# Layer 1's residual, scaled in pieces under the query and gate projections and added in place

## The chip, the cores and the metric

The kernel runs on one core of a Trainium2 chip. The metric is the device time of one execution in microseconds (us). Six actors matter: TensorE (PE; its weight loads are listed apart as PEld), VectorE (DVE), ScalarE (ACT), GpSimd (POOL), SyncE (SP), which here only issues transfers, and the 16 DMA engines that carry them. Each engine runs its own list of instructions in order; engines wait for each other through semaphores.

## The reference

Two layers of a decoder trunk over 256 tokens of width 2048, in float32. Layer 0 is a gated linear recurrence, layer 1 a sparse attention with a gate. Each layer ends alike, with alpha = 4 ** 0.25:

```
h = _layer_norm(alpha * h + mixer(h) @ w_out, ln_g, ln_b)

def _layer_norm(x, g, b):
    mu  = mean(x);  var = mean((x - mu) ** 2)
    return (x - mu) * rsqrt(var + 1e-5) * g + b
```

So layer 1 needs layer 0's output h twice: for its input projection, and again at its end as the residual alpha * h. What is computed of it at the end is `n * l0_ln_g + l0_ln_b`, where n is the normalised value before gain and bias.

In layer 1, `x @ w_in` gives queries (2048 columns), six groups of keys and values (512 columns each), 48 gate logits and the gate z (2048 columns). Queries and keys get a partial rotary embedding. The attention's result is multiplied by silu(z) and goes through `w_out` (2048 x 2048).

## The kernel before

**Tiles.** Tokens lie in two tiles of 128 (t = 0, 1), the width in 16 pieces of 128. A matmul in full precision is three passes: both factors are split into a high part (fp32r) and the remainder, and hi·hi, hi·lo and lo·hi are added (`tok_step`, lines 138 to 142, with 512 columns; `project_t`, lines 185 to 189, with 256). All weights pass once through one stream: `load` (line 105) issues a transfer of 512 KB on SP into a raw slot `wr`; ScalarE writes the high part `wh` (line 78), VectorE the remainder `wl` (line 79); then TensorE uses them. There are three raw slots and five pairs of split buffers, or four and eight while the pool `wide` is open. A raw slot is free again when VectorE has made the remainder. SP's list holds the loads in order, so a load that waits for a slot holds all that stand behind it.

**Stages.** Layer 0 with its norm (which writes n to a tensor `norm0` in DRAM), layer 1's keys and values, then four groups of queries: `query(g)` projects 512 columns, applies `rotary` (line 552: a copy `qr` on ScalarE, four operations on GpSimd, back into `qr`), transposes on TensorE (line 198) and does the attention; `gate(g)` projects 512 columns of z and multiplies. In this stage `wide` is closed. At last the output projection: four groups of 512 columns, the last one token tile by token tile (`project_by_tile`), each followed by `residual` (line 852: hb = alpha * xr + product) and the sums for the norm; then the norm's two steps with l1_ln_g and l1_ln_b and the stores.

**The residual before.** In the output projection, `fetch(c)` (line 820) loads 512 columns of n into `xr` (two buffers), 512 columns of gain and bias into `gb` (one buffer), all issued by SP, and GpSimd multiplies and adds (lines 828 and 829). `row` (line 832) loads l1_ln_g and l1_ln_b, 1 MB each when spread over the 128 partitions. `wide` is opened again after the second group.

**What sets the order.** A scheduler puts every engine's list in order, by a timeline of its own, from the order of the code, priorities (weight splits go up to 300 instructions ahead) and explicit rules such as `issue_after`. So a new transfer or operation can stand elsewhere in the lists than in the code.

## Time and profile before

| | |
|---|---|
| median of 3 runs | 1016.73 us (1016.64 to 1019.19) |
| profiled execution | 1017.92 us, span 1016.2 us |
| granted TensorE clock, mean | 0.994 |
| TensorE busy | 997.0 us |
| VectorE, ScalarE, GpSimd busy | 670.2, 543.9, 116.3 us |
| moved by DMA | 185.25 MB, 182 GB/s in the mean |

The span goes from the first to the last instruction. Queries, gates and attention take about 676 to 905 us of it, the output projection about 905 to 1005, the end behind the last matmul the rest. In rows of the profile a line number stands for the code, `out<-in` for the tiles, `x` for the number of instructions; "A <- B" means that A waited for B. A busy TensorE is not TensorE at its peak, since the ends of matmuls are modelled; starts are measured.

### The profile page before, as it was taken

To read this page: it belongs to the slowest core of one execution; us is meant where nothing else is said; L and a number is where in the kernel's file an instruction comes from. 1 tells how busy PE (TensorE), PEld (TensorE's weight loads), DVE (VectorE), ACT (ScalarE), POOL (GpSimd) and SP (SyncE) were. 2 spreads that over 40 slices of the span, in tenths; PEclk is the share of its full clock that TensorE was granted. 3 is DMA by queue.
4 is the path that set the end of the run, shared out by engine and by line. 5 is a ranking of instruction groups with operands and counts; after the bars stand their busy time and mean duration, and the time that the engine had idled before them with its cause. 6 is when DMAs were issued, how large, how long until landed. Compare 5 with 4: busy or idle time off the path is not lost.

```text
span 1016.2 us, 15908 instructions
## 1 busy us (share of the span) xinstructions
PE 997.0 (98%) x6041; PEld 883.4 (87%) x6041; DVE 670.2 (66%) x1101; ACT 543.9 (54%) x864; POOL 116.3 (11%) x180
## 2 busy tenths in 40 slices
PE   8999999999999999999999999999999999999995
PEld 8988998899889988878889878899989889998775
DVE  6786658665866686656575555466857668675566
ACT  6654455445544554424476545564856667775240
POOL 1400300030003000310011020101010022000540
PEclk9999999999999999999999999999999999999998
DMA  9865565556655655557465677577354454445872
GB/s 304 260 214 166 155 176 178 163 151 178 179 156 153 183 174 162 163 176 258 141 217 175 205 227 230 165 218 212 108 165 144 146 166 130 121 145 184 308 253 83
DMA packets 100781, 185.25 MB, mean 182 GB/s; under 512 B 6097, under 2 KB 20513, under 8 KB 100193
## 3 DMA queue, kind: packets, MB, share of 16 engines
q1 hardware_dynamic: 99232, 178.67, 57.7%
q0 software_dynamic: 1472, 5.56, 1.8%
q8 instruction: 47, 0.77, 0.3%
q14 instruction: 30, 0.24, 0.1%
HBM read 180.02 MB, written 4.19 MB: 181 GB/s over the span
## 4 chain that ended last, share of the span: by engine, by line
PE 86%; DMA 5%; DVE 3%; issue 3%; POOL 2%; ACT 1%; SPq 0%; POOLq 0%; ACTq 0%; DVEq 0%
PE pjb L141 15%; PE pjb L142 15%; PE pjb L140 15%; PE pjb L187 9%; PE pjb L185 9%; PE pjb L188 9%; PE mxb L425 2%; DMA wr<-in_l_w_in_dram 2%; DMA wr<-in_l_w_out_dram 2%; DVE wl L79 1%; PE mxb L198 1%; PE mxb L548 1%; PE mxb L550 1%; PE mxb L549 1%; PE mxb L777 1%
## 5 line engine op out<-in xcount | busy, mean ns | idle before, releaser
L79 DVE TENSOR_TENSOR wl<-wr,wh 128x1024 fp32r<-128x1024 f32 (+2 forms) x330 | 396.4, 1205 | 221.6 <-ACT wh L78 219.0
L78 ACT ACTIVATE wh<-wr 128x1024 fp32r<-128x1024 f32 (+2 forms) x330 | 340.4, 1036 | 350.9 <-PE pjb L142 144.8
L185 PE MATMUL pjb<-ah,wh 128*128 128x256 f32 x832 | 235.4, 284 | 1.2 <-ACT wh L78 1.2
L187 PE MATMUL pjb<-al,wh 128*128 128x256 f32 x832 | 235.7, 284 | 0.0
L188 PE MATMUL pjb<-ah,wl 128*128 128x256 f32 x832 | 234.5, 284 | 0.5 <-DVE wl L79 0.5
L141 PE MATMUL pjb<-wl,ah 128*128 128x512 f32 (+1 forms) x576 | 223.3, 388 | 0.3 <-DVE wl L79 0.3
L140 PE MATMUL pjb<-wh,ah 128*128 128x512 f32 (+1 forms) x576 | 222.8, 387 | 0.0
L142 PE MATMUL pjb<-wh,al 128*128 128x512 f32 (+1 forms) x576 | 222.8, 387 | 0.0
L185 PEld LDWEIGHTS pjb<-ah,wh 128*128 128x128 f32 x832 | 157.0, 189 | 2.2 <-ACT wh L78 1.6
L188 PEld LDWEIGHTS pjb<-ah,wl 128*128 128x128 f32 x832 | 156.2, 189 | 1.2 <-DVE wl L79 1.1
L187 PEld LDWEIGHTS pjb<-al,wh 128*128 128x128 f32 x832 | 156.2, 188 | 0.5
L142 PEld LDWEIGHTS pjb<-wh,al 128*128 128x128 f32 x576 | 109.0, 189 | 22.3
L141 PEld LDWEIGHTS pjb<-wl,ah 128*128 128x128 f32 x576 | 109.0, 189 | 22.0 <-DVE wl L79 0.6
L140 PEld LDWEIGHTS pjb<-wh,ah 128*128 128x128 f32 x576 | 108.9, 189 | 22.0
L141 PE MATMUL pjb<-wl,bh 128*128 128x512 f32 (+1 forms) x272 | 105.1, 386 | 1.4 <-DVE wl L79 1.4
L142 PE MATMUL pjb<-wh,bl 128*128 128x512 f32 (+1 forms) x272 | 104.1, 384 | 0.0
L140 PE MATMUL pjb<-wh,bh 128*128 128x512 f32 (+1 forms) x272 | 103.1, 384 | 0.2 <-ACT wh L78 0.2
L141 PEld LDWEIGHTS pjb<-wl,bh 128*128 128x128 f32 x272 | 51.3, 189 | 13.7 <-DVE wl L79 3.3
L140 PEld LDWEIGHTS pjb<-wh,bh 128*128 128x128 f32 x272 | 51.2, 188 | 11.3 <-ACT wh L78 0.6
L142 PEld LDWEIGHTS pjb<-wh,bl 128*128 128x128 f32 x272 | 51.3, 189 | 10.5
L488 POOL TENSOR_TENSOR gz<-gz,gn 128x512 f32<-128x512 f32 x8 | 13.6, 1697 | 317.4 <-ACT gz L487 316.8
L559 POOL TENSOR_TENSOR rot<-qr,cc 128x128 f32<-128x128 f32 x14 | 9.5, 679 | 275.2 <-ACT qr L555 274.9
(220 smaller groups left out, 1013.8 us busy)
## 6 DMA issues: line engine op xcount, KB each, us to landing
wr<-in_l_w_in_dram SPq DMA_DIRECT2D x230, 512.0 KB, 3.8
wr<-in_l_w_out_dram SPq DMA_DIRECT2D x64, 512.0 KB, 4.3
wr<-in_l_w_in_dram SPq DMA_DIRECT2D x16, 280.0 KB, 3.3
wr<-in_l_cmp_w_k_dram SPq DMA_DIRECT2D x8, 512.0 KB, 4.4
wr<-in_l_cmp_w_v_dram SPq DMA_DIRECT2D x8, 512.0 KB, 4.3
xr<-in_x_dram POOLq DMA_DIRECT2D x4, 512.0 KB, 6.1
norm<-hb POOLq DMA_DIRECT2D x2, 1024.0 KB, 5.4
xr<-norm SPq DMA_DIRECT2D x4, 512.0 KB, 7.4
```

Source lines behind the costliest of these rows:

```text
L78: act.activation(hi, src, AF.Copy)
L79: dve.tensor_tensor(lo, src, hi.bitcast(F32), op=OP.subtract)
L140: pe.matmul(ps, xh, wh, start=(k == 0), stop=False)
L141: pe.matmul(ps, xh, wl, start=False, stop=False)
L142: pe.matmul(ps, xl, wh, start=False, stop=(k == KT - 1))
L185: pe.matmul(o, hi[:, kk, c], xh, start=(k == 0 and b % 2 == 0), stop=False, skip_group_check=True)
L187: pe.matmul(o, hi[:, kk, c], xl, start=False, stop=False, skip_group_check=True)
L188: pe.matmul(o, lo[:, kk, c], xh, start=False, stop=(k == KT - 1), skip_group_check=True)
L198: last[0] = pe.transpose(ps[:, i], src[:, i], ident).ins
L425: pe.matmul(ps[:, h], km[:, h].rearrange("p b r j -> p (b r j)"), later, start=True, stop=True)
L488: pool.tensor_tensor(z, z, gn, op=OP.mult)
L548: pe.matmul(o, a[0], b[0], start=start, stop=False)
```

## The change

Layer 1's residual is now made in eight pieces of 256 columns. A function `rescale` is called in each of the four query and four gate projections, after the third of its eight weight tiles. It takes a raw weight slot, loads 256 columns of n (256 KB) and of gain and bias (128 KB each, spread over the partitions) into it through SP, multiplies and adds on GpSimd, and stores the 256 KB to a new DRAM tensor `res1` by GpSimd's queue. In the output projection, 512 columns at a time of `res1` are loaded straight into `hb`, and `residual` adds in place. `l1_ln_g` and `l1_ln_b` come in four pieces each. All these loads are placed by a table of (column group, weight tile), each to be issued after the weight load named last. `wide` opens after the first group instead of the second. `fetch`, `xr` and `gb` are gone.

```diff
--- before.py
+++ after.py
@@ -66,6 +66,7 @@
     mx = ctx.enter_context(tc.tile_pool(name="mx", bufs=4, space=PSUM))
     dram = ctx.enter_context(tc.tile_pool(name="dram", bufs=1, space=DRAM))
     norm0 = dram.tile([S, D], F32, name="norm0")
+    res1 = dram.tile([S, D], F32, name="res1")
 
     def pjb(shape):
         return pj.tile(shape, F32, name="pjb", tag="pjb")
@@ -99,10 +100,13 @@
         def at(self, k, c):
             return self.hi[k // 4][:, k % 4, c], self.lo[k // 4][:, k % 4, c]
 
+    queued = [None]
+
     def load(w, j, c0, n):
 
         raw = slot([128, 2, n], F32, "wr", 3, 1)
-        nc.sync.dma_start(raw, w[256 * j:256 * (j + 1), c0:c0 + n].rearrange("(k p) n -> p k n", p=128))
+        queued[0] = nc.sync.dma_start(raw, w[256 * j:256 * (j + 1), c0:c0 + n].rearrange(
+            "(k p) n -> p k n", p=128)).ins
         return raw
 
     def weights(w, j, c0, n):
@@ -153,10 +157,14 @@
                 also(j)
         return ps
 
-    def project_by_tile(xs, w, c0, after, behind=None, halve=False):
-
-
-        ws = [weights(w, j, c0, 512) for j in range(KT // 2)]
+    def project_by_tile(xs, w, c0, after, behind=None, halve=False, also=None):
+
+
+        ws = []
+        for j in range(KT // 2):
+            ws.append(weights(w, j, c0, 512))
+            if also:
+                also(j)
         for t in range(NT):
 
             n = 256 if halve and t == NT - 1 else 512
@@ -789,14 +797,30 @@
         act.activation(o, po, AF.Copy)
         return o
 
+    todo = list(range(D // 256))
+
+    def rescale(j):
+
+
+        if j != 2:
+            return
+        u = slice(256 * todo[0], 256 * todo.pop(0) + 256)
+        r = slot([128, 4, 256], F32, "wr", 3, 1)
+        nc.sync.dma_start(r[:, 0:2], norm0[:, u].rearrange("(t p) d -> p t d", p=128))
+        for i, name in enumerate(("l0_ln_g", "l0_ln_b")):
+            nc.sync.dma_start(r[:, 2 + i], a[name][None, u].to_broadcast([128, 256]))
+        for i, op in enumerate((OP.mult, OP.add)):
+            pool.tensor_tensor(r[:, 0:2], r[:, 0:2], r[:, 2 + i, None].to_broadcast([128, 2, 256]), op=op)
+        nc.gpsimd.dma_start(res1[:, u].rearrange("(t p) d -> p t d", p=128), r[:, 0:2])
+
     def query(g):
-        pq = project(hT, w1, C_Q + 512 * g)
+        pq = project(hT, w1, C_Q + 512 * g, rescale)
         q = [rotary(at, t, pq[t]) for t in range(NT)]
         ps = [scores(g, t, q[t]) for t in range(NT)]
         return [values(g, t, ps[t]) for t in range(NT)]
 
     def gate(g, os):
-        for i, ps in enumerate(project_t(hT, w1, C_Z + 512 * g)):
+        for i, ps in enumerate(project_t(hT, w1, C_Z + 512 * g, also=rescale)):
             zT = at.tile([128, 2, S], F32, name="zT", bufs=1)
             act.activation(zT, ps, AF.Silu)
             for t in range(NT):
@@ -817,40 +841,29 @@
     stats = n1.tile([128, NT, 8, 6], F32, name="stats", bufs=1)
 
 
-    def fetch(c):
+
+    g1, b1 = (n1.tile([128, D], F32, name=n, bufs=1) for n in ("g1", "b1"))
+    others = {}
+    for c, at in enumerate(((0, 5), (1, 0), (2, 0), (2, 3))):
         cs = slice(512 * c, 512 * (c + 1))
-        xr = n1.tile([128, NT, 512], F32, name="xr")
-        nc.sync.dma_start(xr, norm0[:, cs].rearrange("(t p) d -> p t d", p=128))
-        gb = n1.tile([128, 2, 512], F32, name="gb", bufs=1)
-        for i, name in enumerate(("l0_ln_g", "l0_ln_b")):
-            nc.sync.dma_start(gb[:, i], a[name][None, cs].to_broadcast([128, 512]))
-        for t in range(NT):
-            pool.tensor_tensor(xr[:, t], xr[:, t], gb[:, 0], op=OP.mult)
-            pool.tensor_tensor(xr[:, t], xr[:, t], gb[:, 1], op=OP.add)
-        return xr
-
-    def row(name):
-        r = n1.tile([128, D], F32, name=name, bufs=1)
-        nc.sync.dma_start(r, a[name][None, :].to_broadcast([128, D]))
-        return r
-
+        others[at] = hb[:, :, cs], res1[:, cs].rearrange("(t p) d -> p t d", p=128)
+        for i, (r, name) in enumerate(((g1, "l1_ln_g"), (b1, "l1_ln_b"))):
+            at = ((2, 5), (2, 7), (3, 0), (3, 1), (3, 2), (3, 3), (3, 5), (3, 7))[2 * c + i]
+            others[at] = r[:, cs], a[name][None, cs].to_broadcast([128, 512])
+
+    def also(c, j):
+        if (c, j) in others:
+            with tc.issue_after(queued[0]):
+                nc.sync.dma_start(*others[c, j])
 
     for c in range(4):
         cs = slice(512 * c, 512 * (c + 1))
 
-        xr = []
-
-        def behind(j, c=c, xr=xr):
-            if j == 3:
-                xr.append(fetch(c))
-
-        def residual(t, ps, c=c, xr=xr, parts=range(2)):
-            xr = xr[0]
+        def residual(t, ps, c=c, parts=range(2)):
             n = ps.shape[1] // len(parts)
             for i, u in enumerate(parts):
                 h = hb[:, t, 512 * c + 256 * u:512 * c + 256 * (u + 1)]
-                dve.scalar_tensor_tensor(h, xr[:, t, 256 * u:256 * (u + 1)], ALPHA, ps[:, n * i:n * (i + 1)],
-                                         op0=OP.mult, op1=OP.add)
+                dve.scalar_tensor_tensor(h, h, ALPHA, ps[:, n * i:n * (i + 1)], op0=OP.mult, op1=OP.add)
                 dve.bn_stats(stats[:, t, 2 * c + u], h)
 
         def finish(t, ps):
@@ -871,16 +884,12 @@
                     nc.sync.dma_start(y[128 * t:128 * (t + 1), gs], h)
 
         if c < 3:
-            for t, ps in enumerate(project(oT, a["l1_w_out"], 512 * c, behind)):
+            for t, ps in enumerate(project(oT, a["l1_w_out"], 512 * c, lambda j, c=c: also(c, j))):
                 residual(t, ps)
-            if c == 2:
-                last_xr = fetch(3)
-            if c == 1:
+            if c == 0:
                 widen()
-                g1, b1 = row("l1_ln_g"), row("l1_ln_b")
         else:
-            xr.append(last_xr)
-            project_by_tile(oT, a["l1_w_out"], 512 * c, finish, halve=True)
+            project_by_tile(oT, a["l1_w_out"], 512 * c, finish, halve=True, also=lambda j: also(3, j))
     wide.close()
 
 
```

Where this puts instructions is shown at three places. Buffer numbers differ between the two programs, since they count what was made before.

SP, from the first query projection on. The raw slots `wr` are numbered by load; behind each row stand the semaphores that it waits for. Before, the fourth load of that projection and the four behind it:

```order
L105 DMA wr_6607<-in_l1_w_in_dram 128x2x512 [waits DMAHW4_49,DVE_49]
L105 DMA wr_6625<-in_l1_w_in_dram 128x2x512 [waits DMAHW5_49,DVE_49]
L105 DMA wr_6643<-in_l1_w_in_dram 128x2x512 [waits DMAHW6_49,DVE_49]
L105 DMA wr_6661<-in_l1_w_in_dram 128x2x512 [waits DMAHW7_49,DVE_49]
L105 DMA wr_6679<-in_l1_w_in_dram 128x2x512 [waits DMAHW0_49,DVE_49]
```

Now, the first rescale (`wr_6608`) in that place, the eight loads up to the second rescale (`wr_7077`), and the load behind it:

```order
L809 DMA wr_6608<-norm0_72 128x2x256 [waits DMASW5_49,DMAHW4_49,DMASW4_49,DVE_49]
L811 DMA wr_6608<-in_l0_ln_g_dram 128x256
L811 DMA wr_6608<-in_l0_ln_b_dram 128x256
L108 DMA wr_6615<-in_l1_w_in_dram 128x2x512 [waits DMAHW5_49,DVE_49]
L108 DMA wr_6633<-in_l1_w_in_dram 128x2x512 [waits DMAHW6_49,DVE_49]
L108 DMA wr_6651<-in_l1_w_in_dram 128x2x512 [waits DMAHW2_49,DVE_49]
L108 DMA wr_6669<-in_l1_w_in_dram 128x2x512 [waits DMAHW0_49,DMAHW1_49,DMASW2_49,Pool_49]
L108 DMA wr_6687<-in_l1_w_in_dram 128x2x512 [waits DMAHW3_49,DVE_49]
L108 DMA wr_6987<-in_l1_w_in_dram 128x2x512 [waits DMAHW7_49,DMAHW4_49,DVE_49]
L108 DMA wr_7017<-in_l1_w_in_dram 128x2x512 [waits DMAHW5_49,DVE_49]
L108 DMA wr_7047<-in_l1_w_in_dram 128x2x512 [waits DMAHW6_49,DVE_49]
L809 DMA wr_7077<-norm0_72 128x2x256 [waits DMAHW7_49,DVE_49]
```

Eight weight loads still stand between one rescale and the next; `wr_6669` waits for GpSimd and its queue, that is for the first rescale's slot, and `wr_6687` to `wr_7077` stand behind it.

GpSimd, at the first query group's rotary. Before:

```order
L559 TENSOR_TENSOR rot_6699<-qr_6697,cc_91 128x128
L560 TENSOR_TENSOR rot_6699<-qr_6697,ss_92 128x4x16
L561 TENSOR_TENSOR rot_6699<-qr_6697,ss_92 128x4x16
L562 TENSOR_TENSOR qr_6697<-rot_6699 128x4x32
L559 TENSOR_TENSOR rot_6706<-qr_6704,cc_91 128x128
L560 TENSOR_TENSOR rot_6706<-qr_6704,ss_92 128x4x16
L561 TENSOR_TENSOR rot_6706<-qr_6704,ss_92 128x4x16
L562 TENSOR_TENSOR qr_6704<-rot_6706 128x4x32
```

Now, with the second rescale and its store:

```order
L813 TENSOR_TENSOR wr_7077<-wr_7077 128x512 x2
L814 DMA res1_73<-wr_7077 128x2x256
L567 TENSOR_TENSOR rot_6707<-qr_6705,cc_92 128x128
L568 TENSOR_TENSOR rot_6707<-qr_6705,ss_93 128x4x16
L569 TENSOR_TENSOR rot_6707<-qr_6705,ss_93 128x4x16
L570 TENSOR_TENSOR qr_6705<-rot_6707 128x4x32
L567 TENSOR_TENSOR rot_6714<-qr_6712,cc_92 128x128
L568 TENSOR_TENSOR rot_6714<-qr_6712,ss_93 128x4x16
```

On ScalarE the copies `qr` that feed this rotary stand, now as before, behind the split of the fourth load of the first gate projection; that load (`wr_7084`) is now the one that SP issues right behind the second rescale:

```order
L79 ACTIVATE wh_7019<-wr_7017 128x1024 [waits DMAHW0_49,DVE_49,PE_49]
L79 ACTIVATE wh_7049<-wr_7047 128x1024 [waits DMAHW1_49,DVE_49,PE_49]
L79 ACTIVATE wh_7086<-wr_7084 128x1024 [waits DMAHW5_49,DVE_49,PE_49]
L563 ACTIVATE qr_6705<-pjb_6552 128x512 [waits DMASW7_49,DMASW0_49,PE_49]
L563 ACTIVATE qr_6712<-pjb_6553 128x512 [waits PE_49]
L79 ACTIVATE wh_7116<-wr_7114 128x1024 [waits DMAHW6_49,DVE_49]
```

Both rescales of the first query group are ahead of its rotary on GpSimd, where nothing was.

SP, in the output projection. Before:

```order
L105 DMA wr<-in_l_w_out_dram 128x2x512 x15
L823 DMA xr<-norm_72 128x2x512
L826 DMA gb<-in_l_ln_g_dram 128x512
L826 DMA gb<-in_l_ln_b_dram 128x512
L823 DMA xr<-norm_72 128x2x512
L834 DMA l_ln_g<-in_l_ln_g_dram 128x2048
L834 DMA l_ln_b<-in_l_ln_b_dram 128x2048
L105 DMA wr<-in_l_w_out_dram 128x2x512 x3
L826 DMA gb<-in_l_ln_g_dram 128x512
L826 DMA gb<-in_l_ln_b_dram 128x512
L823 DMA xr<-norm_72 128x2x512
L105 DMA wr<-in_l_w_out_dram 128x2x512 x3
```

Now:

```order
L108 DMA wr<-in_l_w_out_dram 128x2x512 x16
L857 DMA hb<-res_73 128x2x512 x3
L108 DMA wr<-in_l_w_out_dram 128x2x512 x5
L857 DMA g_9335<-in_l_ln_g_dram 128x512
L108 DMA wr<-in_l_w_out_dram 128x2x512
L857 DMA hb<-res_73 128x2x512
L108 DMA wr<-in_l_w_out_dram 128x2x512 x2
L857 DMA g_9335<-in_l_ln_g_dram 128x512
L108 DMA wr<-in_l_w_out_dram 128x2x512
L857 DMA b_9336<-in_l_ln_b_dram 128x512
L108 DMA wr<-in_l_w_out_dram 128x2x512
L857 DMA b_9336<-in_l_ln_b_dram 128x512
```

One weight load more stands ahead of the residual; three parts of it come together, the fourth later, and the pieces of l1_ln_g and l1_ln_b stand between single weight loads.

## The prediction

> **What bounds the kernel now.** I read the page first, then busy time by stage, then TensorE's and SP's own order of time.
>
> ```profile
> PE 997.0 (98%) x6041; PEld 883.4 (87%) x6041; DVE 670.2 (66%) x1101; ACT 543.9 (54%) x864; POOL 116.3 (11%) x180
> ```
>
> TensorE is idle 19.2 us of 1016.2. What a change can win is what TensorE loses in the stages that it touches. By stage (us, then busy time of PE, PEld, DVE, ACT, POOL, granted clock, DMA share, GB/s):
>
> ```profile
> 676.00:905.00 229.00, 229.00 (x1505) 208.43 (x1504) 163.27 (x362) 155.86 (x354) 20.45 (x32) 1.00 0.52 152
> ```
>
> In the query and gate projections and the attention between them, where work is to be put, TensorE has no idle time at all: there is nothing to win, only to lose. In the output projection it does wait. Its order of time there (start, duration, idle time before it in brackets):
>
> ```profile
> 950.64 0.40 PE L142 MATMUL pjb<-wh,bl 128*128 128x512 f32 x1
> 951.25 0.74 PE L140 MATMUL pjb<-wh,bh 128*128 128x512 f32 x2 [0.21 <-ACT wh L78]
> 952.51 0.50 PE L141 MATMUL pjb<-wl,bh 128*128 128x512 f32 x1 [0.52 <-DVE wl L79]
> 952.85 0.39 PE L142 MATMUL pjb<-wh,bl 128*128 128x512 f32 x1
> ...
> 981.80 0.39 PE L140 MATMUL pjb<-wh,bh 128*128 128x512 f32 x1
> 982.46 0.50 PE L141 MATMUL pjb<-wl,bh 128*128 128x512 f32 x1 [0.27 <-DVE wl L79]
> 982.79 0.40 PE L142 MATMUL pjb<-wh,bl 128*128 128x512 f32 x1
> ...
> 987.94 0.39 PE L140 MATMUL pjb<-wh,bh 128*128 128x512 f32 x1
> 988.80 0.50 PE L141 MATMUL pjb<-wl,bh 128*128 128x512 f32 x1 [0.47 <-DVE wl L79]
> 989.13 0.39 PE L142 MATMUL pjb<-wh,bl 128*128 128x512 f32 x1
> ...
> 990.77 0.28 PE L141 MATMUL pjb<-wl,bh 128*128 128x256 f32 x1
> 991.24 0.50 PE L141 MATMUL pjb<-wl,bh 128*128 128x512 f32 x1 [0.19 <-DVE wl L79]
> 991.58 0.40 PE L142 MATMUL pjb<-wh,bl 128*128 128x512 f32 x1
> ```
>
> Matmuls overlap, so the loss is read from start to start. An undisturbed step is 0.235 us for 512 columns and 0.12 for 256. From 950.64 to 952.85 four matmuls took 2.21 us instead of 0.94: 1.27 lost. Likewise 0.52 (two in 0.99), 0.72 (two in 1.19) and 0.46 (a 256 and a 512 in 0.81). Together **3.0 us**.
>
> Why these weights were late stands in the queue of SP, which issues weight loads (L105), residual parts (L823), their gains and biases (L826) and the two 1 MB rows (L834) in one order:
>
> ```profile
> SPq L826 <- POOL xr L829: 11.3, 3, 5.4
> ...
> 938.32 2.72 SPq L105 DMA_DIRECT2D wr<-in_l_w_out_dram  x3
> ...
> 952.49 3.95 SPq L105 DMA_DIRECT2D wr<-in_l_w_out_dram  x3
> ```
>
> Between 941 and 952 SP issued no weights: it stood behind the single gb buffer, which GpSimd had not given back (11.3 us in three waits), and the three loads issued at 938.32 had 3.5 MB of other transfers ahead of them.
>
> **The change, part by part.**
>
> *Taken from the output projection*: the gb loads with their waits, and GpSimd's work. The 512 KB residual parts stay, as plain loads; the two rows come in eight pieces spread between weight loads. Three residual parts (1.5 MB) stand where 3.5 MB stood, with one weight load more ahead of them, and I see no other wait of SP there. So nearly all of the 3.0 goes: I take 2.7, with bounds 0 (the burst still starves TensorE) and 3.0. The end behind the last matmul is the same chain of VectorE steps and stores: 0.
>
> *In place*: the residual add reads hb instead of xr, in the same shape and number: 0. The wider weight pool comes one column group earlier and issues nothing: 0.
>
> *Added to the query and gate projections*: eight rescales. Each takes one of three raw weight slots, three DMA issues on SP, of which the first waits for a free slot with all later weight loads behind it, two GpSimd operations, and a store on GpSimd's queue. The slot is free only when that store has landed. Two answers of the waits view, for ScalarE (which splits the weights) in 665 to 698 and in 705 to 905, tell where that hurts:
>
> ```profile
> ACT wh L78 <- DMA wr<-in_l_w_in_dram: 11.4, 11, 1.6
> ...
> ACT wh L78 <- PE pjb L142: 16.2, 11, 3.2
> ```
>
> Later, ScalarE waits for TensorE to give back split buffers: weights are ahead, and I cost rescales three to eight at 0. Without that cover each would delay the stream by the 6 us or so that its slot is held longer than a load's. At the first query projection, ScalarE waits for landing loads: there is no cover for the first two. The rows for these (two SP issues; landing of eleven loads, min/median/max us; the two split steps; GpSimd's scaling and DMA issue at their old places, min/median/max ns; DMA rows, median us from issue to landing):
>
> ```profile
> 674.08 0.37 SPq L105 DMA_DIRECT2D wr<-in_l_w_in_dram  x1
> ...
> 676.77 0.37 SPq L105 DMA_DIRECT2D wr<-in_l_w_in_dram  x1
> ...
> DMA to landing us min/median/max: 3.6/4.4/4.7
> ...
> L79 DVE TENSOR_TENSOR wl<-wr,wh x12: 1225/1226/1227, 672.8 to 697.8; 128x1024 fp32r<-128x1024 f32 x12
> ...
> L78 ACT ACTIVATE wh<-wr x11: 1050/1060/1062, 674.4 to 696.7; 128x1024 fp32r<-128x1024 f32 x11
> ...
> L828 POOL TENSOR_TENSOR xr<-xr,gb x8: 1282/1294/3149, 940.0 to 977.5; 128x512 f32<-128x512 f32 x8
> ...
> L510 POOL DMA_DIRECT2D xr<-in_x_dram x4: 722/726/746, 449.0 to 465.0; - x4
> ...
> norm<-hb POOLq DMA_DIRECT2D x2, 1024.0 KB, 5.4
> ...
> out_dram<-hb SPq DMA_DIRECT2D x8, 256.0 KB, 2.3
> ...
> gn<-in_l_g_norm_dram POOLq DMA_DIRECT2D x4, 256.0 KB, 5.5
> ```
>
> The first rescale takes the slot of the load that went out at 674.08. Its three transfers are together as large as a weight load: 0.8 for the two further issues and 4.4 to land (bounds 2.3, the out row, and 4.7). GpSimd's two operations: 2.6 (up to 6.3). The store, 256 KB to DRAM, lies between 2.3 (out, on the other queue, in a quiet time) and 5.5 (the same size on GpSimd's queue): I take 4.0, the middle. The slot is free at 674.1 + 5.2 + 2.6 + 4.0 = 685.9.
>
> A load holds a slot while it lands, 1.06 on ScalarE and 1.23 on VectorE: 5.9 to 7.0; I take 6.4, for fewer loads fly together. By the waits in SP's order this slot then carries two weight loads, `wr_6669` and `wr_7017` (to 698.7), and a third, `wr_7084`, whose split on ScalarE (4.0 + 0.1 + 1.06) ends at 703.9. Behind that split stands the copy qr of the first query group. What hangs on the copy, now:
>
> ```profile
> 698.01 1.29 ACT L555 ACTIVATE qr<-pjb 128x512 f32<-128x512 f32 x2 [0.26 <-PE pjb L142]
> ...
> 698.73 0.59 POOL L559 TENSOR_TENSOR rot<-qr,cc 128x128 f32<-128x128 f32 x1 [41.82 <-ACT qr L555]
> ...
> 699.96 0.46 POOL L562 TENSOR_TENSOR qr<-rot 128x128 f32<-128x128 f32 x1
> ...
> 702.70 0.60 PE L198 MATMUL mxb<-ident,qr 128*128 128x128 f32 x4
> ```
>
> One copy is 0.6 and the rotary's four steps 1.7 (698.73 to 700.42). TensorE takes the result at 702.70, 2.3 us later, and its place in TensorE's order stays. After the change: 703.9 + 0.6 + 1.7 = 706.2, **3.5 late**. The way over GpSimd says the same, since the second rescale now stands ahead of this rotary there. It gets the slot issued at 676.77 after three loads: 676.8 + 3 x 6.4 = 696.0; landed 701.2, scaled 703.8, store issued (0.7) 704.5, rotary done 706.2. With the shortest values (5.9 a load, 2.3 to land) it is 702.6, not late; with the longest (7.0, 4.7, 6.3) about 9 late.
>
> A gap of that length costs more than itself. The trace has one, in the key projection, for a rotary that came late:
>
> ```profile
> 594.76 0.84 PE L198 MATMUL mxb<-ident,qr 128*128 128x128 f32 x4 [2.31 <-POOL qr L562]
> 595.25 0.78 PE L141 MATMUL pjb<-wl,ah 128*128 128x512 f32 x1
> ...
> 598.67 0.39 PE L140 MATMUL pjb<-wh,ah 128*128 128x512 f32 x1
> ...
> 595.00:598.00 3.00, 3.00 (x11) 2.42 (x10) 1.23 (x1) 1.29 (x2) 0.00 (x0) 0.52 0.70 227
> ```
>
> After 2.31 us idle the granted clock stood at 0.52, and the eight matmuls from 595.25 to 598.67 took 3.42 us instead of 1.88. Price **1.5**. The Trainium skill (TensorE: Matmul & The Clock Gate, section Why this matters for your kernels) asks for no idle gap over about 3 us; by that rule the 2.31 would have cost nothing more, and this trace shows that it did. A gap between the two would by the rule save the 1.5, by the trace not.
>
> **Sum.** 3.5 (gap) + 1.5 (clock) - 2.7 (output projection) = **+2.3 us**. The profiled execution took 1017.92 (span 1016.2 and 1.7 around it), so 1020.2 for such a one. The median of the runs is 1016.73, and I forecast **1019.0**. The case's own range: gap 2.3 to 6.5, so +1.1 to +5.3, 1017.8 to 1022.0.
>
> **Rivals.**
>
> *The rotary is hardly late* (not slower, at best faster). Loads and stores land at their shortest, the gap stays under 2.3 and the clock at 1.00: 0 to 2.3, less 2.7 to 3.0, gives 1013.7 to 1016.3. For it, the out row's 2.3; against it, GpSimd's queue at 5.4 and 5.5. It decides where the second rescale is scaled before 702.6. The Trainium skill (DMA: Bandwidth & Descriptors, Anatomy of one DMA) puts a transfer of that queue at 2.0 us and its bytes at 436 GB/s, an estimate of 2.6 for this store, which speaks for this rival; by the same fit 1 MB takes 4.4, where the norm row has 5.4. The section also warns of a long receipt for writes to HBM, which speaks against it.
>
> *Later rotaries wait too.* In the second query group the gate projection's rescale stands ahead of the rotary as well, and the slack is smaller:
>
> ```profile
> 759.27 1.50 POOL L562 TENSOR_TENSOR qr<-rot 128x128 f32<-128x128 f32 x1
> ...
> 761.83 0.60 PE L198 MATMUL mxb<-ident,qr 128*128 128x128 f32 x4
> ```
>
> Done at 760.8, taken at 761.8: 1.0. A gap of 2.5 and its clock drop come on top: +2.3 + 4.0, 1023.0. Against it, the weights are ahead by then, so that rescale is issued early.
>
> *The output projection wins nothing.* The burst of 1.5 MB starves TensorE as the 3.5 MB did: 3.5 + 1.5, 1021.7. Against it, it is less than half, behind one more load.
>
> *The change doesn't do what it says*: SP's order has all eight rescales and no gb load left, so I give it no chance.
>
> **How the numbers follow.** Forecast 0.58, hardly late 0.24, later rotaries 0.11, nothing won 0.07. A difference of 0.3%, 3.05 us, is about what the measurement tells from none. The forecast's range crosses it at a gap of 4.25: of its 0.58, 0.36 go to no difference and 0.22 to slower. Of the second case 0.08 go to faster (no gap, all 3.0 won) and 0.16 to no difference; the last two are slower. Faster 0.08, same 0.52, slower 0.40. The range, 1014.3 to 1022.8, leaves out the best corner of the second case and most of the later rotaries.
>
> **What would show it.** In the changed profile: TensorE's wait for qr near 703, 3 to 4 us, with a granted clock near 0.5 behind it; SP's fourth load behind the first rescale issued near 686; no other wait of TensorE in the attention, and none over 0.2 us in the output projection before its last matmul. It is wrong if TensorE doesn't wait at the first rotary, or waits for wh or wl in the query projections.

## The result, and the profile after

The changed kernel takes **1028.29 us** (median of 5, 1026.83 to 1029.07), before 1016.73 (1016.17 to 1019.19): a ratio of 1.0109, 95% interval 1.0098 to 1.0121. It is 11.6 us slower, where 2.3 were forecast and a range to 1022.8. The profiled execution took 1027.32 (span 1025.6).

The page's first part, and the times by stage (us, then busy time of PE, PEld, DVE, ACT, POOL, granted clock, DMA share, GB/s), from the first query projection to the attention's end:

```profile
PE 998.1 (97%) x6041; PEld 883.5 (86%) x6041; DVE 673.7 (66%) x1101; ACT 543.8 (53%) x864; POOL 117.5 (11%) x188
```

```profile
676.00:720.00 44.00, 37.15 (x210) 32.27 (x209) 21.05 (x33) 18.09 (x23) 10.95 (x14) 0.92 0.65 206
...
720.00:905.00 185.00, 181.42 (x1187) 163.89 (x1187) 135.06 (x301) 126.51 (x307) 36.57 (x42) 1.00 0.54 163
```

TensorE's busy time is as before, and its idle time grew from 19.2 to 27.5 us. Where it had none, it now lacks 6.9 of 44 us around the first rotary and 3.6 of the 185 behind. TensorE's waits, of the whole program:

```profile
PE mxb L206 <- POOL qr L570: 8.3, 3, 6.0
PE mxb L556 <- ACT p L740: 1.9, 1, 1.9
...
PE mxb L777 <- DVE st L760: 0.9, 1, 0.9
PE pjb L145 <- DVE wl L80: 0.9, 2, 0.5
PE pjb L144 <- ACT zT L825: 0.7, 1, 0.7
```

L206 is the transpose behind the rotary (6.0 of it at the first query group, the rest stands in the key projections as before). L556 belongs to the attention of the third query group, L777 to that of the second (counted from 1), L145 to the first query projection, L144 to the output projection. In that last stage the waits for late weights are gone, but a new one of 0.7 for the last gate has come.

**The first rotary.** TensorE, GpSimd and ScalarE in order of time:

```profile
701.85 0.28 PE L195 MATMUL pjb<-al,wh 128*128 128x256 f32 x1
708.10 1.11 PE L206 MATMUL mxb<-ident,qr 128*128 128x128 f32 x4 [5.96 <-POOL qr L570]
```

```profile
702.04 1.26 POOL L813 TENSOR_TENSOR wr<-wr 128x512 f32<-128x512 f32 x1 [0.54 <-DMA wr<-in_l_ln_b_dram]
703.60 0.74 POOL L814 DMA_DIRECT2D res<-wr  x1 [0.30 <-POOL wr L813]
705.10 1.00 POOL L567 TENSOR_TENSOR rot<-qr,cc 128x128 f32<-128x128 f32 x1 [0.76 <-ACT qr L563]
...
706.73 1.31 POOL L570 TENSOR_TENSOR qr<-rot 128x128 f32<-128x128 f32 x1
```

```profile
697.26 1.06 ACT L79 ACTIVATE wh<-wr 128x1024 fp32r<-128x1024 f32 x1 [0.63 <-PE pjb L146]
703.47 1.06 ACT L79 ACTIVATE wh<-wr 128x1024 fp32r<-128x1024 f32 x1 [5.15 <-DMA wr<-in_l_w_in_dram]
704.43 1.07 ACT L563 ACTIVATE qr<-pjb 128x512 f32<-128x512 f32 x2
```

ScalarE stood 5.15 us before the split of one weight, with the qr copies behind it; GpSimd was through with the second rescale at 704.3, hardly earlier. TensorE wanted that weight only at 716.0. Its load had been issued 5.8 us later than its counterpart before (before, then after):

```profile
692.14 0.37 SPq L105 DMA_DIRECT2D wr<-in_l_w_in_dram  x1
```

```profile
697.91 21.33 SPq L108 DMA_DIRECT2D wr<-in_l_w_in_dram  x8
```

The clock behind the gap, in 708 to 711:

```profile
708.00:711.00 3.00, 2.90 (x14) 2.90 (x15) 0.36 (x1) 1.45 (x2) 1.51 (x5) 0.50 1.05 404
```

**The later losses** have two kinds of row. At 786 a step of VectorE, 128x6, that takes 0.17 takes 1.19, just while GpSimd scales (first DVE, then POOL; and that line's min/median/max ns before and after):

```profile
785.52 1.19 DVE L760 TENSOR_TENSOR st<-st,gates 128x6 f32<-128x6 f32 x1
786.75 0.19 DVE L762 TENSOR_TENSOR p<-p,st 128x32 f32<-128x32 f32 x1
786.86 1.85 DVE L769 TENSOR_TENSOR p<-p,st 128x256 f32<-128x256 f32 x2
```

```profile
785.40 2.68 POOL L813 TENSOR_TENSOR wr<-wr 128x512 f32<-128x512 f32 x2 [15.10 <-DMA wr<-in_l_ln_b_dram]
```

```profile
L752 DVE TENSOR_TENSOR st<-st,gates x16: 156/166/168, 715.5 to 910.6; 128x6 f32<-128x6 f32 x16
```

```profile
L760 DVE TENSOR_TENSOR st<-st,gates x16: 154/166/1194, 722.5 to 923.6; 128x6 f32<-128x6 f32 x16
```

At 857 the picture is that of the first rotary: SP has waited for a rescale's store before the next weight load (846 to 854), ScalarE waits for that load, and an attention copy (L740) stands behind the split. TensorE wanted the weight at 868.7.

```profile
SPq L108 <- DMA res<-wr: 6.3, 1, 6.3
```

```profile
857.28 1.06 ACT L79 ACTIVATE wh<-wr 128x1024 fp32r<-128x1024 f32 x1 [3.18 <-DMA wr<-in_l_w_in_dram]
858.25 0.37 ACT L740 ACTIVATE p<-mxb 128x256 f32<-128x256 f32 x1
```

### The profile page after: what moved, and what is told of

It reads as the page before. It is cut to its first block, busy times and chain, and to the rows that moved or that the text cites. A ratio compares the mean times of both kernels' runs of the same rounds, so it can differ in the third digit from the quotient of the medians.

```text
span 1025.6 us, 15965 instructions
## 1 busy us (share of the span) xinstructions
PE 998.1 (97%) x6041; PEld 883.5 (86%) x6041; DVE 673.7 (66%) x1101; ACT 543.8 (53%) x864; POOL 117.5 (11%) x188
## 4 chain that ended last, share of the span: by engine, by line
PE 74%; DMA 11%; DVE 5%; ACT 5%; issue 3%; POOL 1%; SPq 1%; POOLq 0%; ACTq 0%; DVEq 0%
PE pjb L146 13%; PE pjb L145 13%; PE pjb L144 13%; PE pjb L193 9%; PE pjb L196 9%; PE pjb L195 9%; DMA wr<-in_l_w_in_dram 7%; DVE wl L80 3%; ACT wh L79 3%; PE mxb L433 2%; DMA wr<-in_l_ln_b_dram 1%; DMA wr<-in_l_cmp_w_v_dram 1%; PE mxb L206 1%; PE mxb L785 1%; DMA wr<-in_l_cmp_w_k_dram 1%
## 5 line engine op out<-in xcount | busy, mean ns | idle before, releaser
L145 PE MATMUL pjb<-wl,ah 128*128 128x512 f32 (+1 forms) x576 | 222.5, 387 | 0.9 <-DVE wl L80 0.9
L144 PE MATMUL pjb<-wh,ah 128*128 128x512 f32 (+1 forms) x576 | 222.3, 386 | 0.0
L145 PEld LDWEIGHTS pjb<-wl,ah 128*128 128x128 f32 x576 | 108.5, 188 | 23.2 <-DVE wl L80 1.8
L144 PEld LDWEIGHTS pjb<-wh,ah 128*128 128x128 f32 x576 | 108.5, 188 | 21.8
L144 PE MATMUL pjb<-wh,bh 128*128 128x512 f32 (+1 forms) x272 | 104.3, 384 | 0.7 <-ACT zT L825 0.7
L145 PE MATMUL pjb<-wl,bh 128*128 128x512 f32 (+1 forms) x272 | 104.5, 384 | 0.0
L144 PEld LDWEIGHTS pjb<-wh,bh 128*128 128x128 f32 x272 | 51.2, 188 | 11.8 <-ACT zT L825 1.1
L145 PEld LDWEIGHTS pjb<-wl,bh 128*128 128x128 f32 x272 | 51.2, 188 | 10.7
L813 POOL TENSOR_TENSOR wr<-wr 128x512 f32<-128x512 f32 x16 | 22.3, 1394 | 165.6 <-DMA wr<-in_l_ln_b_dram 80.2
```

The lines of the kernel that those rows point to most:

```text
L144: pe.matmul(ps, xh, wh, start=(k == 0), stop=False)
L145: pe.matmul(ps, xh, wl, start=False, stop=False)
L813: pool.tensor_tensor(r[:, 0:2], r[:, 0:2], r[:, 2 + i, None].to_broadcast([128, 2, 256]), op=op)
```

## The experiments

My first theory after the result: a held weight slot makes later loads late, and ScalarE and GpSimd, in their fixed order, then stand before late transfers that nobody needs yet, with steps behind them that TensorE does need. Rivals: GpSimd's work itself, the added transfers, or simply eight rescales at about a microsecond each. Each kernel is the changed one with the edit shown; medians stand beside runs of the kernel before on the same chip (1016.3 to 1016.9), and ratios are to those.

### Each half alone

**out_only**: the rescales are gone.

```diff
-        if j != 2:
-            return
+        return
...
-        others[at] = hb[:, :, cs], res1[:, cs].rearrange("(t p) d -> p t d", p=128)
+        others[at] = hb[:, :, cs], norm0[:, cs].rearrange("(t p) d -> p t d", p=128)
```

> Output projection as after the change, but no rescale at all: the residual is loaded from norm0 without its gain and bias (that part of the computation is left out). If the output projection wins what was forecast (2.7 us, bounds 0 to 3.0) and all the loss is in the query and gate projections, 1014.0 (0.2 to 2.8 us under before), with TensorE's waits there under 1 us in all. If the output projection wins nothing, 1016.7. Every theory that puts the loss into the rescales expects no wait of TensorE for qr at the first query group.

Measured: 1013.92, ratio 0.9975 (0.9966 to 0.9984). The output projection wins 2.4 us; the rescales cost the other 14.4.

**skip_first** and **first_two**: the six later rescales alone, and the first two alone (where rescales are left out, `norm0` is loaded in place of `res1`).

```diff
-        if j != 2:
+        if j != 2 or not todo:
...
+    del todo[:]
     gate(0, query(0))
+    todo[:] = range(2, 8)
```

```diff
-        if j != 2:
+        if j != 2 or len(todo) < 7:
```

> The two rescales of the first query group and its gate are left out (columns 0 to 511 of the residual stay without gain and bias), the six later ones stay. Theory 1, the loss has two places: the first two rescales cost the 1.2 us of late weights at 680 to 690 and the 7.7 us at the first rotary, and the later six cost 4 to 5 us in the attention of groups 2 and 3: 1028.3 - 8.9 = 1019.4. Rival, the first rescale to come makes a late rotary wherever it stands (the gap moves to the next query group): 1026 to 1028. Rival, later rescales cost nothing and what the trace shows there comes from the shift at the first rotary: 1014 to 1015.

> After the change, with the first two rescales in weight slots alone; the six later ones are left out (columns 512 to 2047 of the residual stay without gain and bias). Without any rescale the kernel took 1013.9, without these two 1020.7, with all 1028.3. If the costs add up, the first two are worth 7.6 and this takes 1021.5, with the gap of about 6 us at the first rotary and no loss after 720. If the six later ones cost only because the first two had put the stream behind, the two together make nearly all of it: 1024 or more. If TensorE's wait at the start of the output projection (2.1 us in skip_first, 0.7 without rescales) comes from the last rescales, it is 0.7 here.

Measured: skip_first 1020.72, ratio 1.0044 (1.0028 to 1.0061), with no gap at the first rotary and the later waits as after the change. first_two 1025.07, ratio 1.0079 (1.0066 to 1.0092), with a gap of 5.2 and no wait in the attention. Both, and one_first below, have one wait at the start of the output projection that is 1.4 longer than in the other kernels:

```profile
PE pjb L144 <- ACT zT L825: 2.1, 1, 2.1
```

There TensorE's order came out differently: the attention's last matmul ends 0.5 us ahead of this wait instead of 3.3 in out_only, and the copy of its result stands ahead of the Silu (zT) on ScalarE. So 1.4 of each belongs to neither part. Without it the first two cost 9.8 and the later six 5.4 between medians, in sum 15.2 where both together cost 14.4. The 5.4 is an upper value: in skip_first's profiled execution the clock fell to 0.50 behind that wait, which cost about 1.5 more, and from start to start of its instructions TensorE lost 4.0 more than in out_only in the attention (780 to 870). Either way the two places are separate causes, and the later one isn't an echo of the first. That fells the last rival of skip_first.

### The first rotary

**rotary_first**: only an order is changed. `held` has, from the first gate projection on, the first group's second qr copy and its last rotary step on GpSimd; `hold[0]` is that copy, once the second rescale has been issued.

```diff
+          with tc.issue_after(held[1]) if held[1] else nullcontext():
             pool.tensor_tensor(r[:, 0:2], r[:, 0:2], r[:, 2 + i, None].to_broadcast([128, 2, 256]), op=op)
...
-        with tc.high_priority(AHEAD):
+        with tc.high_priority(AHEAD), tc.issue_after(hold[0]) if hold[0] else nullcontext():
             split(hi, lo, raw)
```

> All eight rescales as after the change, each in its raw weight slot. Only an order differs: in the first gate projection ScalarE takes the splits of the weights behind the second rescale after the first group's two qr copies, and GpSimd scales the second rescale after that group's rotary. Theory 1, ScalarE and GpSimd stood in line behind late transfers that nobody needed yet: the gap of 6.1 us and its 1.6 us of slow clock go, 1028.3 - 7.7 = 1020.6, and slots are held as long as before or longer. Rival, the held slots starve TensorE of weights, and the order only shows where: the gap goes but TensorE then waits for wh or wl in the first gate projection, 1026 or more.

Measured: 1023.54, ratio 1.0067 (1.0053 to 1.008). The gap is gone, but only 4.8 of the 7.7 us that were expected are won: the longest of TensorE's waits in 695 to 760 are now

```profile
PE mxb L557 <- ACT qT L79: 1.8, 2, 0.9
PE mxb L781 <- ACT p L744: 1.1, 1, 1.1
PE mxb L557 <- DVE p L747: 1.0, 1, 1.0
PE mxb L559 <- DVE qT L80: 0.9, 1, 0.9
```

It is neither theory's picture. Pushed behind the copies, the late splits stand between the steps of the attention that follows (one ahead of each of the two qT that TensorE waits for). The order moves a part of the loss to another place and saves the rest.

**one_first**: the first rescale alone.

```diff
+        if j != 2 or len(todo) < 8:
```

> After the change with its first rescale alone, in a weight slot in the first query projection; the other seven are left out (the residual stays without gain and bias). Nothing of a rescale stands ahead of the first rotary on GpSimd between 684 and the rotary, and no second slot is taken. Theory, the stream of weights that one held slot puts back is enough: the fourth load behind it is late, ScalarE's split of a gate weight stands before the qr copies, a gap of 1 to 3.5 us at the first rotary, 1016 to 1019.5. Rival, the second rescale makes the gap: none over 0.5, 1014 to 1015.3.

Measured: 1019.0, ratio 1.0026 (1.0014 to 1.0037), 1017.6 without that 1.4. The gap is 1.49:

```profile
704.20 0.66 PE L206 MATMUL mxb<-ident,qr 128*128 128x128 f32 x4 [1.49 <-POOL qr L570]
```

One held slot, long given back, is enough for a gap; the second rescale makes it from 1.5 to 5 or 6.

**no_arith**: no GpSimd arithmetic, still in weight slots.

```diff
-        for i, op in enumerate((OP.mult, OP.add)):
-            pool.tensor_tensor(r[:, 0:2], r[:, 0:2], r[:, 2 + i, None].to_broadcast([128, 2, 256]), op=op)
```

> After the change, in weight slots, without GpSimd's multiplication and addition (the residual stays without gain and bias). A slot is held while its transfers land, 7.3 us, and is stored, 2.6, instead of 11.6 in all. Theory, the loads and the store make most of the hold: held about 9 to 10, the gap at the first rotary 2.5 to 5 instead of 6.1, 1020 to 1025. Rival, GpSimd's arithmetic (its time in the slot and its place ahead of the rotary) is the root: gap under 1, 1014 to 1016.5.

Measured: 1023.23, ratio 1.0061 (1.0048 to 1.0074). The first slot is held 8.9 us, and yet the gap is as long as ever, above the 2.5 to 5 of the theory:

```profile
707.76 1.11 PE L206 MATMUL mxb<-ident,qr 128*128 128x128 f32 x4 [6.14 <-POOL qr L570]
```

So the arithmetic is not what makes the first gap, and a shorter hold alone doesn't shorten it. The slot was free 2.4 us earlier than after the change, but `wr_7084` went out only 1.3 earlier and took 6.4 us to land instead of 5.5, beside the second rescale's store, which now ran at the same time. What is gone are all waits in the attention behind 720, which this expectation hadn't asked for.

**own_paced**: a buffer of its own, and the three loads, under the line added last, tied behind the same weight load on SP. **own_no_arith** and **own_no_gains** take from it the arithmetic, and the two broadcast loads.

```diff
-        r = slot([128, 4, 256], F32, "wr", 3, 1)
+        r = at.tile([128, 4, 256], F32, name="own_r", bufs=1)
+        with tc.issue_after(queued[0]):
```

> All eight rescales with the same transfers, the same GpSimd steps in the same order, but in a buffer of their own, with their loads tied behind the same weight load on SP: no raw weight slot is held. Theory 1, the held slot is the root (late loads, then splits that block ScalarE): no gap at the first rotary over 0.5 us, the later losses gone but for stretched VectorE steps of under 1 us, 1014 to 1015.5, below before. Rival, GpSimd is the root (the second rescale stands ahead of the first rotary, and its steps stretch VectorE's): a gap of 2 us or more at the first rotary, 1019 or more. Rival, the three added transfers per rescale delay the loads wherever they go: 1018 or more, with ScalarE's waits for landing loads as long as after the change.

> As own_paced (own buffer, no weight slot held), without GpSimd's multiplication and addition: the residual stays without gain and bias, all transfers stay. In own_paced ScalarE still split wr_7084 at 700.7, whose load took 7.6 us behind the second rescale's three transfers, and the qr copies stood behind that. Theory 1, with slots free what is left is the transfers: the gap at the first rotary stays, 2 to 3 us, and the time with it, 1016 to 1017.6. Rival, GpSimd's arithmetic ahead of the rotary is what is left: no gap over 0.5 us, 1013.5 to 1015.

> As own_paced, without the two broadcast loads per rescale: GpSimd multiplies with and adds a tile of ones of its own, so that its two steps stay and the result is not the scaled residual. Half of a rescale's bytes and two of its three loads are gone. Theory 1, the transfers are what is left in own_paced: the loads behind the second rescale land in 4 to 5.5 us instead of 7.6, the gap at the first rotary is under 1 us, 1014 to 1015.5. Rival, GpSimd's arithmetic: the gap stays at 2 to 3 us, 1017 or more.

Measured: 1017.63, ratio 1.001 (0.9998 to 1.0022); 1018.18, ratio 1.0011 (0.9999 to 1.0022); 1015.18, ratio 0.9978 (0.9965 to 0.999). The gaps, in this order:

```profile
705.34 0.66 PE L206 MATMUL mxb<-ident,qr 128*128 128x128 f32 x4 [2.71 <-POOL qr L570]
```

```profile
703.23 0.65 PE L206 MATMUL mxb<-ident,qr 128*128 128x128 f32 x4 [2.24 <-POOL qr L570]
```

```profile
703.08 0.66 PE L206 MATMUL mxb<-ident,qr 128*128 128x128 f32 x4 [0.82 <-POOL qr L570]
```

Each gap is that of one execution: own_paced's runs go from 1015.05 to 1020.72 and the profiled one is the slowest, own_no_arith's from 1015.46 to 1020.33 and the profiled one is the third fastest. The held slots are more than half of the gap at the first rotary (6.0 to 2.7), but not all: by my theory own_paced should have had none. What remains is neither the slots nor the arithmetic but the transfers. The three weight loads behind the second rescale landed, in before (four loads), own_paced and own_no_gains, within (min/median/max us)

```profile
DMA to landing us min/median/max: 4.3/4.4/4.7
```

```profile
DMA to landing us min/median/max: 5.4/6.7/7.6
```

```profile
DMA to landing us min/median/max: 4.0/5.3/6.4
```

and with the broadcasts gone most of the gap goes. The three are together no larger than a weight load. Bytes alone could explain the delay: at 692.1 before, one other weight load was in flight, at 693.0 in own_paced one and the three transfers, half as much again, and 4.4 times 1.5 is 6.6 (an estimate, if landing goes with the bytes in flight). But they are also small pieces; the changed kernel's transfers have, per issue (KB, median us to landing),

```profile
wr<-norm SPq DMA_DIRECT2D x8, 256.0 KB, 2.9
...
wr<-in_l_ln_g_dram SPq DMA_DIRECT2D x8, 128.0 KB, 4.3
wr<-in_l_ln_b_dram SPq DMA_DIRECT2D x8, 128.0 KB, 4.9
```

half the bytes in half as long again. Whether it is the bytes, the broadcast, or the order in which the three were issued, no run tells apart.

**own_buffer**: the own buffer without the tie on SP.

> All eight rescales in a buffer of their own as in own_paced (1017.6), but their loads not tied to a weight load, so that the order is as the scheduler makes it: on GpSimd the third rescale too stands ahead of the first rotary, and the fourth to eighth ahead of the second group's. Each needs the store of the one before it, some 12 us apart. Theory, GpSimd's queue can make the wait as well as ScalarE's: TensorE waits for qr 5 us or more at the first rotary and 5 us or more at the second group's, 1028 or more. Rival, with a free buffer the rescales run so early that GpSimd is done in time: 1014 to 1018.

Measured: 1031.14, ratio 1.0141 (1.0126 to 1.0155), a wait of 8.47 for qr at the first rotary. Here the copies were made in time, and GpSimd was not free:

```profile
699.15 1.06 ACT L563 ACTIVATE qr<-pjb 128x512 f32<-128x512 f32 x2
```

```profile
705.74 0.74 POOL L814 DMA_DIRECT2D res<-own_r  x1 [0.30 <-POOL own_r L813]
706.50 0.47 POOL L567 TENSOR_TENSOR rot<-qr,cc 128x128 f32<-128x128 f32 x1
```

So GpSimd's order alone can make the wait, with a third rescale ahead of the rotary: the second path of the prediction exists, though in the changed kernel both were ready within a microsecond of each other. The second group's rotary was not waited for, against the expectation; a wait of 2.9 for ScalarE's pt, behind a late split, stands there.

### The later losses

no_arith has none; own_paced waits 0.2 us, and loses 1.2 more than before from start to start (780 to 820). Two kernels part the slot from the arithmetic; their edits are shown against no_arith. **stretch_only** is no_arith with GpSimd's two steps put back on other tiles, behind the store (`st`); **hold_only** is no_arith with one more load on GpSimd's queue into the slot ahead of the store.

```diff
-        nc.gpsimd.dma_start(res1[:, u].rearrange("(t p) d -> p t d", p=128), r[:, 0:2])
+        st = nc.gpsimd.dma_start(res1[:, u].rearrange("(t p) d -> p t d", p=128), r[:, 0:2]).ins
+        with tc.issue_after(st):
+            for op in (OP.mult, OP.add):
+                pool.tensor_tensor(side, side, unit[:, 0, None].to_broadcast([128, 2, 256]), op=op)
```

```diff
+        nc.gpsimd.dma_start(r[:, 2], a["l0_ln_g"][None, u].to_broadcast([128, 256]))
-        nc.gpsimd.dma_start(res1[:, u].rearrange("(t p) d -> p t d", p=128), r[:, 0:2])
+        nc.gpsimd.dma_start(res1[:, u].rearrange("(t p) d -> p t d", p=128), r[:, 1:3])
```

> As no_arith (weight slots, no arithmetic in the slot, 1023.2, nothing lost in the attention of groups 3 and 4), with GpSimd's two steps put back on tiles of their own, behind the store's issue: the slot is held as short as in no_arith, GpSimd works as long as after the change, about 4 us later. The residual stays without gain and bias. Theory A, GpSimd's steps make VectorE's steps beside them longer, and that is the later loss: VectorE steps of 0.2 us take 0.8 to 1.2 beside them, and 3 to 5 us come back behind 720, 1026 to 1028. Theory B, the longer hold of the slot is the later loss: long VectorE steps, but TensorE loses under 1 us behind 720, 1022.5 to 1024.5.

> As no_arith, with one more 128 KB load on GpSimd's queue into the slot between the loads and the store, so that the slot is held at least as long as after the change (about 12 us), without any GpSimd arithmetic (the stored data are not the scaled residual). Theory A (VectorE stretched by GpSimd): nothing lost behind 720, no more than 2 us over no_arith, from the first rotary alone, 1023 to 1025. Theory B (the hold): the losses behind 720 are back, 3 to 5 us, and the first gap is longer than 6.3, 1027 or more.

Measured: 1027.32, ratio 1.0099 (1.0084 to 1.0115), and 1031.15, ratio 1.0138 (1.0121 to 1.0155). TensorE's waits from 720 to 880, first of stretch_only:

```profile
PE mxb L206 <- POOL qr L570: 1.3, 1, 1.3
PE mxb L777 <- DVE pcs L766: 0.8, 1, 0.8
PE mxb L777 <- DVE st L760: 0.2, 1, 0.2
```

```profile
PE mxb L556 <- ACT p L740: 3.2, 1, 3.2
```

Both theories hold, each at its place. The stretch brings back the wait for VectorE at 792 (L777), and a new one at a rotary; the hold brings back the wait for ScalarE's copy (L740), longer than after the change, and nothing at 792.

### Place or buffer

**own_late** and **slot_late** make all eight rescales at other places: none before the first rotary, none in the third query projection, two each in the last two gate projections; own_late in an own buffer, slot_late in weight slots, both with the loads tied on SP as in own_paced. `spots` names the projection (the first query's is 0) and the weight load (also from 0) behind which each stands.

```diff
+    stage = [-1]
+    spots = ((1, 6), (2, 2), (3, 2), (5, 2), (6, 1), (6, 5), (7, 1), (7, 5))
...
-        if j != 2:
+        if j == 0:
+            stage[0] += 1
+        if (stage[0], j) not in spots:
             return
```

> All eight rescales in full, in a buffer of their own and paced on SP as in own_paced, but none in the first query projection and in the third: one behind the seventh weight load of the first gate projection, one each in the second query and gate and the fourth query projection, two each in the last two gate projections. Theory 1, held slots cost where weights are not ahead of ScalarE, and added transfers cost where ScalarE waits for landing loads (665 to 698): neither is there, so no gap at the first rotary, and only VectorE's steps stretched by GpSimd's are left, under 1 us in all: 1014 to 1015.3, faster than before. Rival, each rescale costs where it stands, about a microsecond, by its transfers or by GpSimd: 1018 or more.

> All eight rescales in full at the places of own_late (none before the first rotary), but in raw weight slots as the change has it. It tells whether the place or the buffer made own_late fast (1014.1). Theory, a held slot costs in the later groups too, since ScalarE then stands before a split whose load is late with attention steps behind it: the 4 to 7 us that skip_first lost behind 780, less what two better places save, 1017 to 1020, with waits of TensorE for ScalarE's or VectorE's attention steps. Rival, the place alone does it: 1013.5 to 1015, no such waits.

Measured: own_late 1014.07, ratio 0.9967 (0.9951 to 0.9982); slot_late **1013.66**, ratio 0.9969 (0.9957 to 0.9981). Both are faster than the kernel before and the changed one, and as fast as out_only: at these places the rescales are free. The rival was right on slot_late. Its slots are not held less; SP's weight loads waited for stores, in slot_late and after the change,

```profile
SPq L108 <- DMA res<-wr: 40.0, 8, 7.2
```

```profile
SPq L108 <- DMA res<-wr: 26.5, 6, 6.3
```

but nothing that TensorE needs soon stands behind them on ScalarE, and from the first query projection on TensorE's longest wait is 0.6.

## Why the prediction was wrong, point by point

- **The output projection** (taken as 2.7): 2.4 by out_only. Right. The stated "none over 0.2 us" there was not: 0.7 for the last gate is new in all kernels of the change.
- **In place**, costed at nothing: no run shows a cost, and none tests it alone.
- **The first slot's hold** (674.1 to 685.9, 11.8): issued 672.1, free at 683.7, 11.6. Right by luck, since three errors cancelled: the transfers took 7.2 instead of 5.2, over the bound; GpSimd multiplied before the last of them had landed (677.0 to 678.3), so that 1.7 came behind them instead of 2.6; and the store landed in 2.6 instead of 4.0, near the low bound.
- **The gap** (3.5): the mechanism was right, a split of `wr_7084` ahead of the qr copy, with GpSimd's second rescale ready hardly earlier; the size was off, 6.0. From the free slot (2.2 earlier than forecast) the two loads took 7.1 each instead of 6.4 (+1.4), the third was split 6.6 after its issue instead of 5.2 (+1.4), and copy and rotary took 3.6 instead of 2.3 (+1.3): done at 708.0 instead of 706.2, and wanted 0.7 earlier than I had it. These terms were priced from rows without the added transfers and with little of VectorE's work beside the rotary; beside the transfers and VectorE's splits (704.6 to 705.8 and 706.5 to 707.7) both kinds are longer.
- **The clock** (1.5): granted 0.50 behind the gap; from 700 to 720 the matmuls lost 7.8 us from start to start, 6.1 of it the gap itself, so 1.7. Right.
- **"I cost rescales three to eight at 0"**: the step that failed outright, and "no other wait of TensorE in the attention" with it. In the changed kernel TensorE lost 4.8 there (2.1 and 2.7, below); skip_first over out_only says 4.0 from start to start and 5.4 between medians. The row of cover was read rightly, weights were 10 us ahead of TensorE, but it is cover for the weights alone. ScalarE keeps its order (857.28: 3.18 us before a split, the attention's copy right behind it): a split that has to wait for a late load holds the attention step behind it, however early the weight is. And GpSimd's steps, costed only by their place in the slot, lengthen VectorE's (0.17 to 1.19 us at 785.5).
- **Late weights in the first query projection**: two waits of 0.47 and 0.41 for `wl`, named as a sign of being wrong, and not in the sum.
- **The rivals**: "later rotaries wait too" did not come true, only the first is late. "Hardly late" was wrong for this kernel, though its price for the store (2.3 to 2.6) was the better one. "The output projection wins nothing" was wrong.

From start to start of its instructions, as the prediction read it, TensorE lost against before 9.0 us more from 680 to 720, 2.1 from 780 to 820 and 2.7 from 820 to 860, and 1.8 less from 860 on: 12.0, against 11.6 between the medians. In the terms of the sum that is 6.1 for the gap instead of 3.5, 1.7 for the clock instead of 1.5, 1.2 for late weights instead of nothing, 4.8 in the attention instead of nothing, and 1.8 won in the output projection instead of 2.7. The two profiled executions lie 9.4 apart, since in the key and value projections (580 to 660), which the change doesn't touch, this execution of before had lost 2.2 more.

## What to carry to other kernels

Slack is per queue: that TensorE has a weight 10 us early says nothing of the ScalarE instruction that stands behind that weight's split, so for work that delays a stream ask at each place which step stands behind the late one in its engine's order. Work put under another stage is best tried at several places before the buffer is blamed: the same eight rescales in weight slots cost 14 us at one set of places and nothing at another. A price read where an operation runs alone can be too low for it beside the work it is to hide under: here two loads, a third one with its split, and copy with rotary came out 1.3 or 1.4 us dearer each.

## What the hardware showed that I had not expected

- **VectorE and GpSimd lengthen each other.** A 128x6 step of VectorE took 1.19 us instead of 0.17 until GpSimd's step of 1.3 ended, and the rotary's first and last step took 1.00 and 1.31 instead of 0.59 and 0.46 beside VectorE's subtractions. In stretch_only the 128x6 step took 1.84. The Trainium skill (SBUF — State Buffer, section Who interferes with whom) states it as a lock on a shared pair of ports: a VectorE instruction with two SBUF inputs contends with a GpSimd instruction that reads SBUF, and the loser blocks. The steps named here have two SBUF inputs each; the trace agrees.
- **The length of an idle time alone does not tell whether the clock drops.** Behind a wait of 1.91 us the granted clock over the next 3 us was 1.00 in the changed kernel (858.7) and 0.73 in stretch_only (593.9). Behind 2.1 it was 0.50 in skip_first and 1.00 in first_two and one_first, behind 2.16 (slot_late) 0.65, behind 2.24 (own_no_arith) 1.00. Waits of 1.77 (skip_first) and less left it at 1.00; what decides between 1.9 and 2.3 is not shown. Where it drops, these traces have 0.50 for 3.4 us (934.5 to 937.9 in skip_first), or for a multiple of that at the longest waits. The prediction's 2.31 was no threshold, and the 3 us of the Trainium skill (TensorE: Matmul & The Clock Gate, section Why this matters for your kernels) is too generous here.
- **Added loads beside a stream slow it**: in own_paced three transfers with the bytes of one weight load brought the median landing of the loads behind from 4.4 to 6.7 us. Whether their bytes or their small pieces did it is open.
